# Modulation vectors 2 and 3 of the first layer: products in steps of four column groups, set into group A's projection

## The chip, the cores and the metric

One core of a Trainium2 chip. The metric is the device time of one execution in microseconds (us); lower is better. Engines: TensorE (PE; its weight loads PEld), VectorE (DVE), ScalarE (ACT), GpSimd (POOL), and SyncE (SP), on whose queue every load and store is issued, in order.

## What is computed

A two-layer transformer backbone over 512 latent tokens with 256 context tokens, width 1024, all in float32. Each layer has a mixing part (one projection whose columns feed three groups: A, a gated MLP; B, differential attention with q, k and v; C, a convolution) and a gated convolutional feed-forward part. Six modulation vectors steer a layer (shift, scale and gate, twice), for two streams: latent (`c`) and context (`c_ctx`).

```python
def adaln(cvec, w, b, n):
    m = jax.nn.silu(cvec) @ w[:, : n * D_MODEL] + b[: n * D_MODEL]
    return jnp.split(m, n, axis=-1)
...
sh1, sc1, g1, sh2, sc2, g2 = [m[:, None, :] for m in adaln(c, w_mod[l], b_mod[l], 6)]
hl = modulate(rms_norm(x_lat, norm1_g[l]), sh1, sc1)
pa, q, k, v, pc = project(hl, P, rope)
...
x_lat = x_lat + g1 * mixer_merge(pa, o, pc, P, lam_init)
h2 = modulate(rms_norm(x_lat, norm2_g[l]), sh2, sc2)
```

Vectors 0 and 1 (shift and scale of the mixing part) are needed before the projection; vector 2 (its gate `g1`) first where the output projection is added to `x`; vector 3 (shift of the second part) later still.

## The kernel before

The whole kernel is one program under a tile framework: the code names tiles, and a scheduler sets each engine's order from priorities and dependences. An engine then runs its queue in order. `low(n)` lowers the priority of what is written inside it, `tc.high_priority` raises it.

**Projections.** A matrix product in full precision is three products of rounded halves: weights and activations are split into hi and lo (`wsplit`, L215: ScalarE rounds to hi, VectorE or GpSimd subtracts for lo; `hhi`, `hlo` are the split activations). `proj_tok` (L435) projects all tokens onto 512 columns. It goes through four chunks (`k2`) of the contraction; each has two weight tiles `wh`, `wl`, and for six token tiles 24 products with `wh` (L443, L444) and then 12 with `wl` (L451), into six accumulators `acc`. After each token tile of either half it counts a step (12 a chunk, 48 in all) and calls the hooks given for that step. In the first layer the order is: group C (L486), A (L523), K, Q, V. There are two buffers each for `wh` and `wl` and three for the raw weights.

**Modulation vectors of the first layer.** `mod_rows` (L148) makes up to four pieces of 128 outputs at once on TensorE: the silu of `c` and `c_ctx` is the stationary operand `cs`, 32 columns wide (two used), the modulation weights `mraw` stream past. The eight contraction slices k go to four column groups of the array, and the results lie on four strips of 32 partitions of the accumulator `mr`:

```python
def part(o, k, w):
    r = 32 * (k % 4)
    T.matmul(o[r:r + 32], cs[:, k], w, start=k < 4, stop=k >= 4, tile_position=(0, r))
```

ScalarE copies `mr` to `mrow` (L171); four small products with `sel` (L176, tile `mt`) add the strips and turn the row into columns, and VectorE adds the bias (L181, `modv`). Vectors 0 and 1 are made in pieces of 128 columns ahead of the projection (`piece`). Vectors 2 and 3 are made behind group C in the code, in four halves of 512 columns (eight products of 512 columns, four loads of 512 KB each), under `low(RLOW)` with `RLOW = 250`: the scheduler sets each of their products among others, where it finds place. The four `mraw` buffers (`MRB`) are shared with the split weights of group A's gate (`wsh`, `wsl`, both named wmraw in the trace).

**Group A behind its projection.** ScalarE applies the gelu (L97, tiles `u`, `v`), VectorE takes mean and variance of `v` (L536), ScalarE normalises (L547), VectorE scales and shifts (L548, L549), ScalarE rounds `vbh` (L550) and VectorE makes `vbl`. `a_finish` (L553), called by hooks of K's projection, multiplies by the gate weights (tile `pg`: L275 with `vbh`, L276 with `vbl`), VectorE makes `yA` (L559), TensorE transposes it (`pt`), and ScalarE and VectorE split it.

**Beside it.** VectorE works through the convolution of group C, 60 steps (L701, tile `cacc`), at low priority. Behind K's projection it normalises and rotates the keys (`qk_tile`, from L606), splits them (`ks`), and TensorE transposes them (`pk`, L631) at hooks of Q's projection.

Of the kernel before, what the change touches and what calls it, by code (L numbers as in the profile page):

```python
# [9 lines left out]
F32 = mybir.dt.float32  # L10
# [6 lines left out]
P = 128  # L17
DM = 1024
KD = DM // P
# [10 lines left out]
COL_A, COL_Q, COL_K, COL_V, COL_C = 0, 512, 1024, 1536, 2048  # L30
# [11 lines left out]
NOSYNC = mybir.DependencyInfo(mybir.DependencyClass.NoSync, mybir.DependencyReason.DATA)  # L42
# [6 lines left out]
MRB, MRW, RAWB, NSQ, NTB, KXB, FTB = 4, 2, 3, 2, 3, 3, 2  # L49

HP, SCP, RSP = 1000, 2, 60
DLOW, RLOW = 150, 250
CLOW = (4000, 1000)

WE = "dpdpdpdddppdpppppddp"
# [21 lines left out]
def tile_backbone(  # L77
# [6 lines left out]
    nc = tc.nc  # L84
    V, S, G, T = nc.vector, nc.scalar, nc.gpsimd, nc.tensor
# [16 lines left out]
    def low(n):  # L102
        return tc.high_priority(offset=-n)
# [44 lines left out]
    def mod_rows(cs, sel, chunks, ps, tag, bufs, rp, rtag, rb):  # L148


        n = len(chunks)
        acc = ps.tile([P, 4, P], F32, tag=tag, name="mr", bufs=bufs)

        def part(o, k, w):
            r = 32 * (k % 4)
            T.matmul(o[r:r + 32], cs[:, k], w, start=k < 4, stop=k >= 4, tile_position=(0, r))  # L156

        if chunks[0][0] < 2:
            for c, (i, f) in enumerate(chunks):
                raw = rp.tile([P, KD, P], F32, tag=rtag, name="mraw", bufs=rb)  # L160
                nc.sync.dma_start(out=raw, in_=w_modN[i, f])
                for k in range(KD):
                    part(acc[:, c], k, raw[:, k])
        else:
            for k2 in range(KD // 2):
                raw = rp.tile([P, 2, 512], F32, tag=rtag, name="mraw", bufs=rb)
                nc.sync.dma_start(out=raw, in_=w_modH[chunks[0][0] - 2, chunks[0][1] // 4, k2])
                for a in range(2):
                    part(acc.rearrange("p c q -> p (c q)"), 2 * k2 + a, raw[:, a])
        mrow = rp.tile([P, 4, P], F32, tag="mrow", name="mrow", bufs=MRW)  # L170
        S.copy(mrow[:, :n], acc[:, :n])  # L171

        def finish():
            tr = ps.tile([P, 4, 2], F32, tag=tag, name="mt", bufs=bufs)
            for c in range(n):
                T.matmul(tr[:, c], mrow[:, c], sel, start=True, stop=True)  # L176
            for i in sorted({i for i, f in chunks}):
                cl = [c for c in range(n) if chunks[c][0] == i]
                f0, f1 = chunks[cl[0]][1], chunks[cl[-1]][1] + 1
                src = tr[:, cl[0]:cl[-1] + 1:(cl[1] - cl[0] if len(cl) > 1 else 1)]  # L180
                V.tensor_add(modv[:, 0, :, i, f0:f1], src.rearrange("p f s -> p s f"),  # L181
                             bmod[:, 0, i, f0:f1].unsqueeze(1).to_broadcast([P, 2, f1 - f0]))

        return finish
# [147 lines left out]
    for l in range(DEPTH):  # L332
        last = l == DEPTH - 1
        NT_KV = NLT + NCT
        NT = NLT if last else NLT + NCT
# [23 lines left out]
        with ExitStack() as ph:  # L359
            sac = ExitStack()  # L360
            sp = pool(sac, f"s1_{l}", side)
            ps = psum_pool(ph, f"ps1_{l}")
# [7 lines left out]
            def wchunk(col, k2, **kw):  # L370
                tags = ("raw", "raw") if k2 % 2 else ("hi", "lo")
                return wsplit_of(("in", col, k2), wsrc(col, k2), [2, 512], wengine(col, k2), tags, **kw)

            if l == 0:
                cs = sp.tile([P, KD, 32], F32, name="cs")
# [109 lines left out]
                    T.matmul(o.rearrange("p a n -> p (a n)"), z[:, :P], z, start=True, stop=False)  # L485
            for k2 in range(KD // 2):  # L486
                wh, wl = wchunk(COL_C, k2, raw=pre.get(k2))
                for a in range(2):
                    k = 2 * k2 + a
                    for s in range(nseg)[::-1]:  # L490
                        t0, t1 = SEG[s]
                        for m in range(4):
                            ms = slice(m * P, (m + 1) * P)
                            o = pc[s][m][:, :t1 - t0]
                            T.matmul(o, wh[:, a, ms], hhi[:, k, t0:t1], start=k == 0 and s == 0, stop=False)
                            T.matmul(o, wh[:, a, ms], hlo[:, k, t0:t1], start=False, stop=False)  # L496
                            T.matmul(o, wl[:, a, ms], hhi[:, k, t0:t1], start=False,
                                     stop=k == KD - 1 and (s == 0 or m % 2 == 1))
# [5 lines left out]
            for s in range(nseg):  # L504
                n = SEG[s][1] - SEG[s][0]
                o0 = PAD if s == 0 else 2 * PAD + LAT
                for c in range(2):
                    sg = sp.tile([P, 512], F32, tag="nsq", name="csg", bufs=2 if l else NSQ)
                    act(sg[:, :n], pc[s][2 + c][:, :n], AF.Sigmoid)
                    V.tensor_mul(cin[:, c, o0:o0 + n], pc[s][c][:, :n], sg[:, :n])  # L510
            if l == 0:
                with low(RLOW):
                    fin = []
                    for i in (2, 3):
                        for f in (0, 4):
                            fin.append(mod_rows(cs, sel, [(i, f + x) for x in range(4)], ps, "aux", 2, sp, "mraw", MRB))
                            if len(fin) > 1:
                                fin.pop(0)()
                    for f in fin:
                        f()  # L520


            pa = proj_tok(COL_A, range(NT))  # L523
            u = sp.tile([P, NT, AW], F32, name="u")
            v = sp.tile([P, NT, AW], F32, name="v")
            mv = sp.tile([P, NT, 2], F32, name="mv")
# [648 lines left out]
```

## Time and profile before

| | us |
|---|---|
| median of three runs | 1602.82 (1602.46 to 1603.99) |
| the profiled execution | 1602.73 |
| its span in the profile | 1600.4 |
| TensorE busy in it | 1565.2 |
| VectorE busy | 1016.0 |
| ScalarE busy | 643.3 |
| GpSimd busy | 113.3 |

The time is that of a whole execution; the span runs from the first to the last recorded instruction. Busy time is the union of an engine's instructions, so products that overlap count once. In a timeline row the first number is the start and the second the duration; what stands in brackets is the idle time ahead of it and what ended it. TensorE's ends are modelled, so what a product costs is read from one start to the next.

### The profile page before, as it was taken

What the parts mean: (1) busy time and instruction counts of PE and PEld (TensorE: products, weight loads), DVE (VectorE), ACT (ScalarE), POOL (GpSimd) and SP (SyncE); (2) the same over time, 40 slices, a digit from 0 to 9 for tenths busy, and PEclk for the clock granted to TensorE, in tenths of its full rate; (3) what the DMA queues carried; (4) which work ended last, traced back from release to release, by engine and by line L of the source; (5) the groups of instructions that cost most, each with busy time, mean ns of one, the idle gap of its engine ahead of it and who ended that gap; (6) DMA issues with size and microseconds to landing.
All of it is one profiled execution on the core that took longest, in us unless ns stands there. A gap on an engine that the chain in (4) does not pass through costs nothing.

```text
span 1600.4 us, 21118 instructions
## 1 busy us (share of the span) xinstructions
PE 1565.2 (98%) x8186; PEld 1289.8 (81%) x8186; DVE 1016.0 (63%) x1713; ACT 643.3 (40%) x1115; POOL 113.3 (7%) x128
## 2 busy tenths in 40 slices
PE   6999998999999999999999999999999999999999
PEld 4875776778788888888888887887778888888888
DVE  4497968969999982145444354996977444334433
ACT  5431568762532221124333233255765333123321
POOL 1130124310000000000000000001320000000000
PEclk9999999999999999999999999999999999999999
DMA  7625210015265872116666476642011323332232
GB/s 282 216 68 183 62 54 27 14 40 198 68 196 185 284 257 74 63 66 198 209 192 207 152 272 221 202 157 93 14 42 54 103 95 96 89 103 92 92 108 90
DMA packets 76372, 208.77 MB, mean 130 GB/s; under 512 B 11504, under 2 KB 13808, under 8 KB 76144
## 3 DMA queue, kind: packets, MB, share of 16 engines
q1 hardware_dynamic: 76272, 207.43, 40.0%
q8 instruction: 64, 1.05, 0.3%
q14 instruction: 36, 0.29, 0.1%
HBM read 183.28 MB, written 24.12 MB: 130 GB/s over the span
## 4 chain that ended last, share of the span: by engine, by line
PE 91%; DVE 4%; ACT 4%; issue 1%; DMA 0%; POOL 0%; POOLq 0%; DVEq 0%; SPq 0%; ACTq 0%
PE pp L276 13%; PE pp L275 13%; PE pp L277 13%; PE pd L277 6%; PE pd L276 6%; PE pd L275 6%; PE acc L443 5%; PE acc L451 5%; PE acc L444 5%; PE po L870 3%; PE wo L275 2%; PE wo L276 2%; PE wo L277 2%; PE mr L156 2%; ACT e L97 1%; PE accC L496 1%
## 5 line engine op out<-in xcount | busy, mean ns | idle before, releaser
L220 ACT CAST whi<-raw 128x1024 fp32r<-128x1024 f32 (+1 forms) x174 | 178.4, 1027 | 510.3 <-PE pp L276 248.4
L276 PE MATMUL pp<-hlo,whi 128*128 128x512 f32 (+1 forms) x1072 | 380.6, 356 | 0.8 <-DVE hlo L316 0.8
L275 PE MATMUL pp<-hhi,whi 128*128 128x512 f32 (+1 forms) x1072 | 379.8, 356 | 1.5 <-ACT whi L220 1.3
L277 PE MATMUL pp<-hhi,wlo 128*128 128x512 f32 (+1 forms) x1072 | 379.0, 355 | 0.0
L106 DVE TENSOR_TENSOR wlo<-raw,whi 128x1024 fp32r<-128x1024 f32 (+2 forms) x159 | 191.4, 1206 | 287.9 <-ACT whi L220 280.3
L275 PEld LDWEIGHTS pp<-hhi,whi 128*128 128x128 f32 x1072 | 201.3, 188 | 35.2 <-ACT whi L220 2.7
L276 PEld LDWEIGHTS pp<-hlo,whi 128*128 128x128 f32 x1072 | 201.4, 188 | 32.8 <-DVE hlo L316 1.5
L277 PEld LDWEIGHTS pp<-hhi,wlo 128*128 128x128 f32 x1072 | 201.7, 188 | 30.9
L277 PE MATMUL pd<-gh,wlo 128*128 128x512 f32 (+1 forms) x550 | 193.2, 351 | 0.0
L276 PE MATMUL pd<-gl,whi 128*128 128x512 f32 (+1 forms) x550 | 192.5, 350 | 0.0
L275 PE MATMUL pd<-gh,whi 128*128 128x512 f32 (+1 forms) x550 | 191.8, 349 | 0.0
L275 PEld LDWEIGHTS pd<-gh,whi 128*128 128x128 f32 x550 | 103.4, 188 | 15.0
L276 PEld LDWEIGHTS pd<-gl,whi 128*128 128x128 f32 x550 | 103.3, 188 | 15.1
L277 PEld LDWEIGHTS pd<-gh,wlo 128*128 128x128 f32 x550 | 103.7, 189 | 14.4
L701 DVE SCALAR_TENSOR_TENSOR cacc<-cin,cw,cacc 128x783 f32<-128x783 f32 (+1 forms) x120 | 103.4, 913 | 3.4 <-ACT cacc L696 3.4
L1037 DVE TENSOR_TENSOR ft<-ft,pp 128x256 f32<-128x256 f32 (+1 forms) x66 | 39.4, 598 | 95.9 <-PE pp L277 84.4
L192 DVE CUSTOM_DVE_ANT_0 mraw<-mraw,csil,bmod 128x1024 f32<-128x1024 f32 x64 | 81.7, 1279 | 7.2 <-DMA mraw<-in_w_modT_dram 7.1
L97 ACT ACTIVATE ft<-ft 128x768 f32<-128x768 f32 (+1 forms) x44 | 32.6, 740 | 112.4 <-DVE ft L1032 112.3
L443 PE MATMUL acc<-whi,hhi 128*128 128x512 f32 x192 | 77.7, 405 | 0.0
L444 PE MATMUL acc<-whi,hlo 128*128 128x512 f32 x192 | 77.0, 401 | 0.0
L97 ACT ACTIVATE e<-pss,mx 128x768 f32<-128x768 f32 (+1 forms) x80 | 65.1, 816 | 16.8 <-DVE mx L825 15.0
L825 DVE TENSOR_REDUCE mx<-pss 128x1 f32<-128x768 f32 (+1 forms) x80 | 67.3, 845 | 5.6 <-PE pss L823 4.6
(218 smaller groups left out, 2522.1 us busy)
## 6 DMA issues: line engine op xcount, KB each, us to landing
raw<-in_w_gv_dram SPq DMA_DIRECT2D x88, 512.0 KB, 3.2
mraw<-in_w_modT_dram SPq DMA_DIRECT2D x64, 512.0 KB, 4.3
raw<-in_w_down_dram SPq DMA_DIRECT2D x34, 512.0 KB, 3.6
wh<-in SPq DMA_DIRECT2D x24, 512.0 KB, 4.7
wl<-in SPq DMA_DIRECT2D x24, 512.0 KB, 4.5
raw<-in_w_in_dram SPq DMA_DIRECT2D x20, 512.0 KB, 3.9
araw<-in_w_in_dram SPq DMA_DIRECT2D x40, 256.0 KB, 3.6
in<-ahi SPq DMA_DIRECT2D x40, 256.0 KB, 4.7
```

Source lines behind the costliest of these rows:

```text
L97: r = S.activation(out, in_, func, **kw)
L106: (eng or V).tensor_sub(o, a, hi.bitcast(F32))
L192: r = V.tensor_tensor_reduce(out=junk, in0=w, in1=csil[:, s], scale=1.0, scalar=bmod[:, l, i, f:f + 1], op0=ALU.mult, op1=ALU.add, accum_o ...
L220: S.copy(hi, raw)
L275: T.matmul(o, lhi, rhi, start=start, stop=False)
L276: T.matmul(o, lhi, rlo, start=False, stop=False)
L277: T.matmul(o, llo, rhi, start=False, stop=stop)
L443: T.matmul(pt[t], hhi[hs], wh[:, a], start=k2 + a == 0, stop=False)
L444: T.matmul(pt[t], hlo[hs], wh[:, a], start=False, stop=False)
L451: T.matmul(pt[t], hhi[hs], wl[:, a], start=False, stop=k2 + 1 == KD // 2 and a == 1)
L701: V.scalar_tensor_tensor(out=cacc[:, c, :cn], in0=cin[:, c, j:j + cn], scalar=cw[:, l, c, j:j + 1], in1=cacc[:, c, :cn], op0=ALU.mult, op1 ...
L825: V.tensor_reduce(out=mx, in_=pss[:, :nk * P], op=ALU.max, axis=AX.X, negate=True)
```

## The change

Vectors 2 and 3 get a generator, `mod_groups`, with eight steps: two vectors, two halves of 512 columns, two halves of the contraction. A step issues four products, one for each column group, from group 3 to group 0, the last three tied behind the first, and then the loads of the step after next. After the second step of a half, ScalarE copies the accumulator (`mod_turn`, the former end of `mod_rows`), and the turning products come at the end of the next step. The generator is started, with the loads of two steps, before the last chunk of group C; the steps are hooks of group A's projection at its steps 1, 6, 12, ... 42, and the last turning at 47. `low(RLOW)` is gone. The bodies of `mod_turn` and of the copy, `mt` and `modv` are as they were.

```diff
-DLOW, RLOW = 150, 250
+DLOW = 150
+MH = (1, 6, 12, 18, 24, 30, 36, 42, 47)
...
+    def mod_groups(cs, sel, ps, tag, bufs, rp, rtag, rb):
+        todo = [(i, f, k0) for i in (2, 3) for f in (0, 4) for k0 in (0, 4)]
+        raws = {}
+        def load(x):
+            if x < len(todo):
+                i, f, k0 = todo[x]
+                raws[x] = [rp.tile([P, 2, 512], F32, tag=rtag, name="mraw", bufs=rb) for a in range(2)]
                 for a in range(2):
-                    part(acc.rearrange("p c q -> p (c q)"), 2 * k2 + a, raw[:, a])
+                    nc.sync.dma_start(out=raws[x][a], in_=w_modH[i - 2, f // 4, k0 // 2 + a])
+        load(0)
+        load(1)
+        yield
+        fin = None
+        for x, (i, f, k0) in enumerate(todo):
+            if k0 == 0:
+                acc = ps.tile([P, 512], F32, tag=tag, name="mr", bufs=bufs)
+            r = raws.pop(x)
+            head = None
+            for k in (3, 2, 1, 0):
+                c = slice(32 * k, 32 * k + 32)
+                m = T.matmul(acc[c], cs[:, k0 + k], r[k // 2][:, k % 2], start=k0 == 0, stop=k0 == 4,
+                             tile_position=(0, 32 * k))
+                if head is not None:
+                    tc.add_manual_dep(m.ins, head.name, NOSYNC, reason="next to one another")
+                head = head or m.ins
+            load(x + 2)
+            if fin:
+                fin()
+                fin = None
+            if k0 == 4:
+                fin = mod_turn(acc.rearrange("p (c q) -> p c q", q=P), [(i, f + y) for y in range(4)],
+                               sel, ps, tag, bufs, rp)
+            yield
+        fin()
+        yield
...
                 wh, wl = wchunk(COL_C, k2, raw=pre.get(k2))
+                if l == 0 and k2 == 3:
+                    mg = mod_groups(cs, sel, ps, "aux", 2, sp, "mraw", MRB)
+                    next(mg)
...
-            if l == 0:
-                with low(RLOW):
-                    fin = []
-                    for i in (2, 3):
-                        for f in (0, 4):
-                            fin.append(mod_rows(cs, sel, [(i, f + x) for x in range(4)], ps, "aux", 2, sp, "mraw", MRB))
-                            if len(fin) > 1:
-                                fin.pop(0)()
-                    for f in fin:
-                        f()
-            pa = proj_tok(COL_A, range(NT))
+            pa = proj_tok(COL_A, range(NT), [] if l else [(x, lambda: next(mg)) for x in MH])
```

How it moves the order. In the rows below, lines of the changed program are 32 to 40 higher than before (L483, L484 and L491 are L443, L444 and L451).

TensorE, the first accumulator of mr. Before, at the end of K's first chunk (`wlo_1054`), its products stand singly or by three among ordinary ones:

```order
L451 MATMUL acc_1048<-wlo_1054,hhi_93 128x512 x2
L156 MATMUL mr_710<-mraw_711,cs_106 32x512
L451 MATMUL acc_1049<-wlo_1054,hhi_93 128x512
L156 MATMUL mr_710<-mraw_715,cs_106 32x512
L451 MATMUL acc_1049<-wlo_1054,hhi_93 128x512
L156 MATMUL mr_710<-mraw_715,cs_106 32x512
L156 MATMUL mr_710<-mraw_719,cs_106 32x512 x2
L451 MATMUL acc_1050<-wlo_1054,hhi_93 128x512
L156 MATMUL mr_710<-mraw_723,cs_106 32x512
```

Now, at the end of A's first chunk (`wlo_727`), the third step with the four turning products of the half before it:

```order
L491 MATMUL acc_722<-wlo_727,hhi_93 128x512 x2
L491 MATMUL acc_723<-wlo_727,hhi_93 128x512 x2
L192 MATMUL mr_785<-mraw_740,cs_106 32x512 x2
L192 MATMUL mr_785<-mraw_739,cs_106 32x512 x2
L216 MATMUL mt_794<-sel_107,mrow_771 128x2 x4
L483 MATMUL acc_718<-whi_802,hhi_93 128x512
```

The eight products of a half now stand in two steps, the second right behind the chunk's last ordinary products. Only the first step is split, one product ahead of A's first and three behind its first token tile.

TensorE, group A's gate. Before, in the second half of K's third chunk (`wlo_1182`):

```order
L451 MATMUL acc_1047<-wlo_1182,hhi_93 128x512 x2
L451 MATMUL acc_1048<-wlo_1182,hhi_93 128x512 x2
L451 MATMUL acc_1049<-wlo_1182,hhi_93 128x512
L275 MATMUL pg_1082<-vbh_1027,wmraw_1041 128x384
L276 MATMUL pg_1082<-vbl_1028,wmraw_1041 128x384
L277 MATMUL pg_1082<-vbh_1027,wmraw_1042 128x384
L275 MATMUL pg_1091<-vbh_1027,wmraw_1041 128x384
L276 MATMUL pg_1091<-vbl_1028,wmraw_1041 128x384
L277 MATMUL pg_1091<-vbh_1027,wmraw_1042 128x384
```

Now the first two gate products stand right behind K's second chunk (`wlo_1140`), ahead of the third (`whi_1181`); those with `vbl` follow 15 ordinary products later:

```order
L491 MATMUL acc_1049<-wlo_1140,hhi_93 128x512 x2
L491 MATMUL acc_1050<-wlo_1140,hhi_93 128x512 x2
L315 MATMUL pg_1073<-vbh_1027,wmraw_1041 128x384
L315 MATMUL pg_1082<-vbh_1027,wmraw_1041 128x384
L483 MATMUL acc_1045<-whi_1181,hhi_93 128x512
L484 MATMUL acc_1045<-whi_1181,hlo_94 128x512
```

The gate begins 24 products and more earlier in K, with all its products for `vbl` still behind it.

VectorE, convolution steps up to the statistics of v (BN_STATS). Before:

```order
L701 SCALAR_TENSOR_TENSOR cacc_98<-cin_99,cw_72,cacc_98 128x783 x16
L106 TENSOR_TENSOR wlo_1054<-raw_1051,whi_1053 128x1024
L701 SCALAR_TENSOR_TENSOR cacc_98<-cin_99,cw_72,cacc_98 128x783 x6
L536 BN_STATS st6_1003<-v_985 128x6
L536 BN_STATS st6_1006<-v_985 128x6
```

Now, from the first convolution step on; `mt_794` and `mt_861` are the turning products of the first two halves:

```order
L733 SCALAR_TENSOR_TENSOR cacc_98<-cin_99,cw_72,cacc_98 128x783 x6
L108 TENSOR_TENSOR wlo_870<-raw_867,whi_869 128x1024
L221 TENSOR_TENSOR modv_67<-mt_794,bmod_68 128x2x4
L733 SCALAR_TENSOR_TENSOR cacc_98<-cin_99,cw_72,cacc_98 128x783 x11
L221 TENSOR_TENSOR modv_67<-mt_861,bmod_68 128x2x4
L733 SCALAR_TENSOR_TENSOR cacc_98<-cin_99,cw_72,cacc_98 128x783 x9
L108 TENSOR_TENSOR wlo_1054<-raw_1051,whi_1053 128x1024
L108 TENSOR_TENSOR wmraw_1042<-raw_1039,wmraw_1041 128x512
L221 TENSOR_TENSOR modv_67<-mt_924,bmod_68 128x2x4
L733 SCALAR_TENSOR_TENSOR cacc_98<-cin_99,cw_72,cacc_98 128x783 x7
L568 BN_STATS st6_1003<-v_985 128x6
```

Three of the four bias additions now stand ahead of the statistics, and six more convolution steps. From K's norm on, VectorE's order is the one before.

On SP's queue the first four loads of mraw now stand behind C's last weights and ahead of the constants and of A's first weights; the other twelve stand between the weights of A and of K.

## Rows read from the trace of the kernel before

**Rows 1.** The page, part 4: chain that ended last, share of the span by engine
```profile
PE 91%; DVE 4%; ACT 4%; issue 1%; DMA 0%; POOL 0%; POOLq 0%; DVEq 0%; SPq 0%; ACTq 0%
```

**Rows 2.** Stretch 77.78 to 168.53 us: busy time and instructions of each engine
```profile
77.78:168.53 90.75, 90.75 (x394) 59.91 (x393) 78.54 (x96) 26.14 (x45) 17.35 (x4) 1.00 0.38 123
```

**Rows 3.** Tile mr: duration min/median/max in ns, first and last start, forms
```profile
L156 PEld LDWEIGHTS mr<-mraw,cs x320: 106/110/173, 11.6 to 150.8; 128*32 128x32 f32 x160
L156 PE MATMUL mr<-mraw,cs x320: 272/273/617, 11.6 to 151.2; 128*32 128x128 f32 x128, 128*32 128x512 f32 x32
```

**Rows 4.** Timeline, TensorE: start, duration (us), then line, tile, shape, count
```profile
72.49 1.05 PE L156 MATMUL mr<-mraw,cs 128*32 128x512 f32 x2
73.47 0.51 PE L443 MATMUL acc<-whi,hhi 128*128 128x512 f32 x1
...
104.38 2.96 PE L451 MATMUL acc<-wlo,hhi 128*128 128x512 f32 x12
107.18 0.39 PE L443 MATMUL acc<-whi,hhi 128*128 128x512 f32 x1
```

**Rows 5.** Timeline, TensorE: three successive stretches of the first accumulator
```profile
116.14 1.04 PE L156 MATMUL mr<-mraw,cs 128*32 128x512 f32 x2
...
117.55 1.06 PE L156 MATMUL mr<-mraw,cs 128*32 128x512 f32 x6
...
118.96 1.04 PE L156 MATMUL mr<-mraw,cs 128*32 128x512 f32 x2
```

**Rows 6.** Timeline, TensorE: a pair in the second accumulator, between ordinary products
```profile
122.83 0.40 PE L443 MATMUL acc<-whi,hhi 128*128 128x512 f32 x1
123.16 1.05 PE L156 MATMUL mr<-mraw,cs 128*32 128x512 f32 x4
...
124.48 0.39 PE L443 MATMUL acc<-whi,hhi 128*128 128x512 f32 x1
```

**Rows 7.** Timeline, TensorE: a piece of the first two vectors
```profile
42.66 0.95 PE L176 MATMUL mt<-sel,mrow 128*128 128x2 f32 x8
43.54 0.65 PE L156 MATMUL mr<-mraw,cs 128*32 128x128 f32 x16
44.11 0.39 PE L496 MATMUL accX<-hlo,whi 128*128 128x256 f32 x1
```

**Rows 8.** Timeline, TensorE: turning products between ordinary ones
```profile
126.81 0.28 PE L176 MATMUL mt<-sel,mrow 128*128 128x2 f32 x2
...
127.26 0.28 PE L176 MATMUL mt<-sel,mrow 128*128 128x2 f32 x2
```

**Rows 9.** Timeline, ScalarE: first v of group A, and vbh
```profile
105.73 0.38 ACT L97 ACTIVATE v<-acc 128x256 f32<-128x256 f32 x1
...
126.73 1.47 ACT L550 CAST vbh<-v 128x1536 fp32r<-128x1536 f32 x1 [4.70 <-DVE v L549]
```

**Rows 10.** Timeline, VectorE, from group A's projection to K's norm
```profile
83.65 15.20 DVE L701 SCALAR_TENSOR_TENSOR cacc<-cin,cw,cacc 128x783 f32<-128x783 f32 x16
...
107.79 0.74 DVE L536 BATCH_NORM_STATS2 st<-v 128x6 f32<-128x256 f32 x2
...
121.83 3.15 DVE L701 SCALAR_TENSOR_TENSOR cacc<-cin,cw,cacc 128x783 f32<-128x783 f32 x1
...
130.46 1.75 DVE L106 TENSOR_TENSOR vbl<-v,vbh 128x1536 fp32r<-128x1536 f32 x1
...
168.53 1.27 DVE L606 TENSOR_REDUCE rk<-qsq 128x8 f32<-128x512 f32 x2
```

**Rows 11.** Timeline, TensorE: first gate product, K's last chunk, first K transposes
```profile
152.91 0.42 PE L275 MATMUL pg<-vbh,wmraw 128*128 128x384 f32 x1
...
164.76 2.96 PE L451 MATMUL acc<-wlo,hhi 128*128 128x512 f32 x12
...
176.54 0.68 PE L631 MATMUL pk<-identr,ks 128*128 128x128 f32 x6 [0.66 <-DVE ks L106]
```

**Rows 12.** DMA issues, first 200 us: KB each, median us to landing
```profile
mraw<-in_w_modH_dram SPq DMA_DIRECT2D x16, 512.0 KB, 3.9
```

More of the change, by code (lines that the diff above doesn't have):

```diff
@@ L156, in part @@
             T.matmul(o[r:r + 32], cs[:, k], w, start=k < 4, stop=k >= 4, tile_position=(0, r))
[L158 to L167, printed above, removed]
-                for a in range(2):
-                    part(acc.rearrange("p c q -> p (c q)"), 2 * k2 + a, raw[:, a])
+        for c, (i, f) in enumerate(chunks):
+            raw = rp.tile([P, KD, P], F32, tag=rtag, name="mraw", bufs=rb)
+            nc.sync.dma_start(out=raw, in_=w_modN[i, f])
+            for k in range(KD):
+                part(acc[:, c], k, raw[:, k])
@@ new lines, in mod_rows @@
+        return mod_turn(acc, chunks, sel, ps, tag, bufs, rp)
+    def mod_groups(cs, sel, ps, tag, bufs, rp, rtag, rb):
[5 more added lines that the diff above has]
+                raws[x] = [rp.tile([P, 2, 512], F32, tag=rtag, name="mraw", bufs=rb) for a in range(2)]
+                for a in range(2):
+                    nc.sync.dma_start(out=raws[x][a], in_=w_modH[i - 2, f // 4, k0 // 2 + a])
[25 more added lines that the diff above has]
+        yield
@@ L170, in mod_rows, with mod_turn @@
+    def mod_turn(acc, chunks, sel, ps, tag, bufs, rp):
+        n = len(chunks)
         mrow = rp.tile([P, 4, P], F32, tag="mrow", name="mrow", bufs=MRW)
```

## Prediction

> **What bounds the kernel now.** I read the chain that ended last first: 91% of it is TensorE, one long queue of products with hardly a gap [rows 1]. So a change pays if it shortens TensorE's own queue, unless a wait opens in its place. The table by stretches says the same of the place in question, from the first convolution step to K's norm (77.78 to 168.53 us, group A's projection and K's): TensorE is busy for all 90.75 us, while VectorE is idle for 90.75 - 78.54 = 12.2 us [rows 2]. The products of vectors 2 and 3 (tile mr) stand inside this stretch, so what they take is paid in full. I then read the timeline of TensorE for what one costs, and those of ScalarE and VectorE for who would be late next.
>
> **What the 32 products cost now.** The tile's view has their 512-column form; one product is two instructions [rows 3]. Ordinary products follow one another at (107.18 - 104.38) / 12 = 0.233 us [rows 4]. In the first accumulator a stretch of mr stands between single ordinary products: from one stretch to the next it is 117.55 - 116.14 = 1.41 us with one product in the stretch, and 118.96 - 117.55 = 1.41 us with three (x6 is six instructions) [rows 5]. Less the ordinary product, a stretch costs 1.41 - 0.233 = 1.18 us, whether it holds one product or three. A pair costs the same: from 122.83 to 124.48 us stand two ordinary products and one pair, 1.65 - 0.47 = 1.18 us [rows 6]. What costs is therefore the stretch, not the product: products in different column groups run side by side. Before, the order has 18 stretches: six of the first accumulator (the one at 72.49 us ahead of A's first product [rows 4], five around 114 to 121 us) and four pairs in each of the other three. 18 x 1.18 = 21.2 us.
>
> **What they cost after.** Nine stretches: seven of four products, and the first step split into one and three. That four run side by side is shown by the first vectors' pieces: 16 instructions, eight products of 128 columns in two rounds over the four groups, stand from 43.54 to 44.11 us, 0.57 us [rows 7]; a 512-column product alone holds 73.47 - 72.49 = 0.98 us [rows 4], so a quarter of it, twice, is 0.49 us. I take 1.18 us for a four: 9 x 1.18 = 10.6 us. **Products: -10.6 us.** Bounds for a fourth product in a stretch: nothing (as the second and third), or its two weight loads unhidden, 2 x 110 ns [rows 3], over eight stretches 1.8 us.
>
> The Trainium skill, page "TensorE: Matmul & The Clock Gate", section "Measured speedup vs the span model", speaks against full overlap: three column groups gave 2.38 times the speed of one, four row groups 3.07 times. By that a stretch of three would take 1.26 times as long as a single one, and a four (an estimate from that page) 4 / 3.07 x 0.98 = 1.28 us, 0.3 us more, or 2.4 us less gain. The trace does not agree for three: 1.41 us with three, 1.41 us with one.
>
> **The turning products (mt).** Sixteen, now mostly alone between ordinary ones: 127.26 - 126.81 = 0.45 us from one to the next, 0.22 us beyond the ordinary product [rows 8], 16 x 0.22 = 3.5 us. After, four runs of four; a piece's run takes 43.54 - 42.66 = 0.88 us [rows 7], 3.5 us. **No change.** Their input (a ScalarE copy) has 2.3 us or more of ordinary products as cover; where that cover failed, a run would wait about a microsecond.
>
> **Where A and K end.** A now takes 107.18 - 73.47 = 33.7 us with no mr inside. After, it holds eight stretches (9.4 us) and four mt runs (3.5 us) and ends at 120.1 us, T below. K now runs from 107.18 to 164.76 + 12 x 0.233 = 167.6 us [rows 4, 11], 60.4 us; freed of 17 stretches (20.1) and the mt (3.5) it takes 36.8 us and would end at 156.9 us, 10.7 us earlier, if nothing waited.
>
> **The new wait.** Group A's gate (pg) needs vbh, then vbl. Now pg starts at 152.91 us, 46 us after A's end, and waits for nothing [rows 11]. After, its first products stand right behind K's second chunk, two chunks of 36 products after A, at T + 2 x 36 x 0.233 = T + 16.8 us. The trace of before has vbh finished (126.73 + 1.47 = 128.2 us) 21.0 us after A's end and vbl (132.2 us) 25.0 us after [rows 9, 10]. Kept like that, TensorE would wait 4.2 us. But part of the lag was VectorE's backlog of convolution steps (cacc, 15.20 / 16 = 0.95 us each): the statistics of v began 0.6 us after A's end though ScalarE made the first v at 105.73 us [rows 9, 10]. After, with A 12.9 us longer, VectorE does 33 of them ahead of the statistics instead of 27 and is there when the first v is, some 2.5 us before T. What stays is 5 steps between, and a GpSimd split of K's weights that stretches a step (3.15 us at 121.83 us against 0.95 [rows 10]). ScalarE also has the fourth K chunk's rounding ahead of vbh, which waits for K's second hi half at T + 14. I get vbh at T + 16.6 with no stretched step and T + 19 with two: a wait of 0 to 2.4 us, 1.9 taken. vbl then comes 0.5 us late behind its 15 covering products, and yA and pt, three VectorE steps later, 0.4 us. **Waits: +2.8 us**, bounds 0 and 5.1 (4.2 + 0.5 + 0.4).
>
> **VectorE behind it.** From K's end on VectorE sets the pace: the first pk waits for it, 0.66 us at 176.54 us [rows 11]. So its own start on K's norm (168.53 us [rows 10]) has to move too. Up to there it does the same work after as before. Of that time 12.2 us were idle [rows 2]. After, it stands in order behind mt: it has 6 steps and a split from 77.78 us and is at the first modv at 84.7 us, whose mt ends at 86.4 (1.7 us idle); 11 steps later at 97.0 us for 98.1 (1.1); and up to 1.5 us where w_s waits for its buffer in the mraw ring. 4.3 us idle, so it gets there 7.9 us earlier at most. TensorE's 10.7 - 2.8 = 7.9 us and these 7.9 meet; where two such limits meet a little is lost, 0.5 us taken (0 to 2). **+0.5 us.**
>
> **Loads.** The 16 mraw loads move into A, two steps ahead of use: 8.4 us of A's products and two stretches, about 10 us, against 3.9 us to land [rows 12]. The first four now stand ahead of the constants and A's first weights on SP's queue and wait for the last pieces (until about 50 us), so those loads start some 7 us later, near 58 us; A starts at 73.5. No price, at worst 2 us at A's start, where VectorE's first split would be late.
>
> **Sum.** -10.6 + 2.8 + 0.5 = -7.3 us against the profiled execution's 1602.73 us, which is 0.09 us below the median shown: **1595.4 us**. Everything behind the first layer's Q projection keeps its order and moves along. A difference under 0.2% (3.2 us) cannot be told from none here.
>
> **Rivals.**
> A. No wait opens: 1592.1 us. For it: VectorE's earlier start on v. Against it: five steps stand in front of vbh and GpSimd's split falls among them. 0.12.
> B. The fours overlap partly (+1.8), or the chain to vbh keeps its 21 us (+2.3): 1597.2 to 1599.5 us. The page's rule above would belong here. 0.14.
> C. VectorE keeps most of its 12.2 us idle in new places, so that K's norm starts about when it did: 1599.5 us to no change. It needs idle time over 9 us; the two modv waits would have to be three times what I worked out. 0.10.
> D. Slower: the fours, whose order runs from group 3 down to 0, do not run side by side at all. 32 x 0.98 + 9 x 0.2 (the rest of a stretch's 1.18) = 33.2 us against 21.2: +12 us, about 1615 us. The change loses from a stretch of (21.2 - 3.3) / 9 = 2.0 us on. Against it: the stretch of three, and the pieces' 0.57 us. 0.04.
> E. The change does not do what it says: the fours are torn apart by other products. The order of the program shows only the first step torn (1 + 3), and that is in the sum.
>
> **Numbers.** My case, a gain of 5.5 to 9 us, has 0.60. Faster by over 0.2% are it, A and B: 0.86; within 0.2% C: 0.10; slower D: 0.04. The range runs from below A's 1592.1 to where C begins and a little beyond: 1591.8 to 1600.4 us.
>
> **What would show it.** In the changed kernel's profile: mr in nine stretches near 1.2 us each; A ending near 120 us; TensorE waiting for vbh at pg, 1 to 3 us; VectorE waiting for mt twice; K's norm starting near 161 us; pk waiting for VectorE as before. A stretch above 1.5 us, a pg wait above 4 us, or a wait at A's start would make it wrong.

## The result and the profile after

| | before | the change |
|---|---|---|
| median, us | 1602.88 (4 runs, 1602.46 to 1603.99) | 1593.86 (4 runs, 1593.64 to 1595.43) |
| the profiled execution, us | 1602.73 | 1593.64 |
| its span, us | 1600.4 | 1591.9 |

The ratio is 0.9945, 95% interval 0.9928 to 0.9962: faster, with the whole interval beyond the 0.2% (3.2 us) that cannot be told from no change. The forecast was 1595.4 us, the range 1591.8 to 1600.4. With the two later sets of runs of the same kernel the change has 13 runs, median 1594.45 us (1593.64 to 1596.18), and the kernel before 36 beside them, median 1602.49: 8.0 us less, against the 7.3 of the sum; the three sets by themselves give 9.0, 6.9 and 8.2 us. A run of 4377.39 us, of the later gate in experiment 5, is left out of every median and ratio.

TensorE's timeline in the changed kernel: start, duration, line, tile, shape, count, as in [rows 4].

```profile
80.89 3.06 PE L491 MATMUL acc<-wlo,hhi 128*128 128x512 f32 x12
...
91.56 1.07 PE L192 MATMUL mr<-mraw,cs 128*32 128x512 f32 x8
92.56 3.06 PE L491 MATMUL acc<-wlo,hhi 128*128 128x512 f32 x12
...
119.69 0.40 PE L483 MATMUL acc<-whi,hhi 128*128 128x512 f32 x1
```

A stretch of four products (x8, eight instructions) holds TensorE from 91.56 to 92.56, 1.00 us, where a single product held it 0.98 us [rows 4]. From the twelve products with `wlo` of one chunk to those of the next (a sweep) it is 92.56 - 80.89 = 11.67 us, with 36 ordinary products (8.40 us), two stretches and one run of mt in it. There are nine stretches, the first step torn into one and three, and K's first product comes at 119.69 us: group A ends where the prediction put it, at 120.

Then K and the gate, in the same view; what stands in brackets is the idle time ahead of the instruction and what ended it.

```profile
138.80 0.61 PE L315 MATMUL pg<-vbh,wmraw 128*128 128x384 f32 x2 [2.15 <-ACT vbh L582]
...
140.64 0.63 PE L484 MATMUL acc<-whi,hlo 128*128 128x512 f32 x1
141.07 0.63 PE L483 MATMUL acc<-whi,hhi 128*128 128x512 f32 x1
...
144.29 0.34 PE L316 MATMUL pg<-vbl,wmraw 128*128 128x384 f32 x1
...
160.65 0.40 PE L483 MATMUL acc<-whi,hhi 128*128 128x512 f32 x1
```

TensorE waits 2.15 us for vbh at pg; vbl comes in time. What the prediction did not have are the rows from 140 to 143.5 us: successive products start 141.07 - 140.64 = 0.43 us apart instead of 0.23. The table by stretches shows what goes with it. Its columns are the length, then busy time and instructions of PE, PEld, DVE, ACT and POOL, then TensorE's granted clock, DMA share and GB/s. The change first, then the kernel before:

```profile
140.00:142.00 2.00, 2.00 (x7) 1.54 (x6) 2.00 (x3) 0.00 (x0) 0.00 (x0) 0.53 0.00 0
...
254.00:256.00 2.00, 2.00 (x12) 1.63 (x13) 1.99 (x5) 1.85 (x8) 1.24 (x2) 1.00 0.00 0
```

```profile
140.00:142.00 2.00, 2.00 (x10) 0.76 (x9) 2.00 (x4) 0.01 (x1) 0.00 (x0) 1.00 0.45 137
...
254.00:256.00 2.00, 1.20 (x5) 1.24 (x6) 0.97 (x4) 1.79 (x7) 1.24 (x3) 0.50 0.00 0
```

In this execution the granted clock fell to 0.5, the 1.2 GHz level, about a microsecond behind the end of the wait; before, it was 1.00 there. About 255 us, at the start of the first attention, it is the other way round. Both places are taken up below.

VectorE and ScalarE between A's projection and K's norm, and the table for that stretch, beside [rows 10], [rows 9] and [rows 2]:

```profile
85.96 0.17 DVE L221 TENSOR_TENSOR modv<-mt,bmod 128x8 f32<-128x8 f32 x1 [0.70 <-PE mt L216]
...
97.64 0.17 DVE L221 TENSOR_TENSOR modv<-mt,bmod 128x8 f32<-128x8 f32 x1 [1.11 <-PE mt L216]
...
119.33 0.17 DVE L221 TENSOR_TENSOR modv<-mt,bmod 128x8 f32<-128x8 f32 x1 [0.26 <-PE mt L216]
...
120.22 3.00 DVE L733 SCALAR_TENSOR_TENSOR cacc<-cin,cw,cacc 128x783 f32<-128x783 f32 x1
...
132.35 3.17 DVE L733 SCALAR_TENSOR_TENSOR cacc<-cin,cw,cacc 128x783 f32<-128x783 f32 x1
135.44 1.75 DVE L581 TENSOR_TENSOR v<-v,lnv 128x1536 f32<-128x1536 f32 x1
...
144.83 1.14 DVE L591 SCALAR_TENSOR_TENSOR yA<-pg,bst,u 128x384 f32<-128x384 f32 x2 [1.06 <-PE pg L317]
...
161.31 1.27 DVE L638 TENSOR_REDUCE rk<-qsq 128x8 f32<-128x512 f32 x2
```

```profile
137.28 1.47 ACT L582 CAST vbh<-v 128x1536 fp32r<-128x1536 f32 x1 [2.29 <-DVE v L581]
```

```profile
77.78:161.31 83.53, 81.38 (x389) 60.26 (x388) 77.63 (x96) 25.33 (x45) 12.04 (x4) 0.98 0.37 128
```

VectorE waits for mt three times (0.70, 1.11, 0.26 us), two of its convolution steps are stretched to 3.00 and 3.17 us beside GpSimd's splits, and vbh follows the second of them. VectorE is now idle for 83.53 - 77.63 = 5.9 us, 1.06 of it at yA, behind the slow products. It starts K's norm at 161.31 instead of 168.53 us.

### The profile page after: what moved, and what is told of

It is laid out like the page before. It is cut to its first block, busy times and chain, and to the rows that moved or that the text cites. A ratio compares the mean times of both kernels' runs of the same rounds, so it can differ in the third digit from the quotient of the medians.

```text
span 1591.9 us, 21110 instructions
## 1 busy us (share of the span) xinstructions
PE 1555.6 (98%) x8186; PEld 1287.7 (81%) x8186; DVE 1015.4 (64%) x1713; ACT 643.0 (40%) x1115; POOL 108.0 (7%) x128
## 4 chain that ended last, share of the span: by engine, by line
PE 75%; DVE 2%; ACT 1%; issue 0%; POOLq 0%; DVEq 0%; ACTq 0%
PE pp L316 13%; PE pp L315 13%; PE pp L317 13%; PE pd L315 6%; PE pd L317 6%; PE pd L316 6%; PE acc L483 2%; PE acc L484 2%; PE acc L491 2%; PE wo L315 2%; PE wo L316 2%; PE wo L317 2%; PE po L902 1%; PE accC L540 0%; PE accC L538 0%; PE accC L539 0%
## 5 line engine op out<-in xcount | busy, mean ns | idle before, releaser
L483 PE MATMUL acc<-whi,hhi 128*128 128x512 f32 x192 | 78.5, 409 | 0.0
L484 PE MATMUL acc<-whi,hlo 128*128 128x512 f32 x192 | 76.6, 399 | 0.0
```

The costliest lines, as they stand in the source:

```text
L483: T.matmul(pt[t], hhi[hs], wh[:, a], start=k2 + a == 0, stop=False)
L484: T.matmul(pt[t], hlo[hs], wh[:, a], start=False, stop=False)
```

## The experiments

**Theory:** what costs is the stretch, 1.17 us whatever it holds of up to four products, so nine fewer stretches give the gain, less the new wait at the gate. **Rivals:** the products cost, not the stretches; the new place of the products gives the gain; VectorE's queue sets the pace behind A, so that what TensorE saves is partly lost there.

**1. The change once more.** No edit.

> The changed kernel as it is, for a second profile. Two pieces of its gain are not yet told apart: 7.3 us that are there when K's norm begins (the fewer stretches, less the gate's wait), and 1.65 us that come later, where the kernel before ran at half the granted clock from 252 to 260 us and the changed one did not. If that clock piece belongs to the program's timing, this profile shows full clock there again and a time near 1593.9 us. If it is chance from execution to execution, the profile may show half clock at the start of the attention, and the span is then some 1.6 us longer (about 1593.5 instead of 1591.9).

Measured: 1595.48 us (1594.34 to 1596.18), ratio 0.9956 (0.9941 to 0.997). Its profile is the cleaner one to hold against the sum:

```profile
73.44 0.50 PE L483 MATMUL acc<-whi,hhi 128*128 128x512 f32 x1
...
139.31 0.62 PE L315 MATMUL pg<-vbh,wmraw 128*128 128x384 f32 x2 [2.15 <-ACT vbh L582]
139.77 0.39 PE L483 MATMUL acc<-whi,hhi 128*128 128x512 f32 x1
140.00 0.40 PE L484 MATMUL acc<-whi,hlo 128*128 128x512 f32 x1
...
143.03 0.39 PE L483 MATMUL acc<-whi,hhi 128*128 128x512 f32 x1
143.40 0.44 PE L316 MATMUL pg<-vbl,wmraw 128*128 128x384 f32 x1
...
159.88 0.40 PE L483 MATMUL acc<-whi,hhi 128*128 128x512 f32 x1
...
168.53 0.59 PE L663 MATMUL pk<-identr,ks 128*128 128x128 f32 x5
```

```profile
144.21 1.13 DVE L591 SCALAR_TENSOR_TENSOR yA<-pg,bst,u 128x384 f32<-128x384 f32 x2
...
160.54 1.27 DVE L638 TENSOR_REDUCE rk<-qsq 128x8 f32<-128x512 f32 x2
```

```profile
140.00:142.00 2.00, 2.00 (x10) 1.64 (x9) 2.00 (x3) 0.00 (x0) 0.00 (x0) 1.00 0.00 0
...
248.00:250.00 2.00, 2.00 (x8) 1.64 (x7) 1.58 (x7) 1.39 (x5) 0.47 (x1) 0.50 0.00 0
```

The wait for vbh is the same 2.15 us, but behind it products follow at 140.00 - 139.77 = 0.23 us, and VectorE does not wait at yA. Here the clock falls where it fell before the change, at the start of attention. Counted from A's first product:

| us | before | the change | once more |
|---|---|---|---|
| A's first product at | 73.47 | 72.91 | 73.44 |
| K's first product | +33.71 | +46.78 | +46.76 |
| K's last product ends | +94.09 | +87.74 | +86.44 |
| K's norm on VectorE | +95.06 | +88.40 | +87.10 |
| first pk | +103.07 | +96.39 | +95.09 |
| span | 1600.4 | 1591.9 | 1592.6 |

Two profiles with the clock fall in the same place differ by 7.96 us at K's norm, 7.98 at the first pk and 7.8 in the span: the whole gain is made between A's start and K's norm, and kept. In the first profile of the change the fall behind the gate costs 88.40 - 87.10 = 1.3 us, and its lead over before grows from 168.53 - 161.31 = 7.2 us to 350.63 - 341.65 = 9.0 us (an ACT table load in both), because there the attention starts at full clock. The second is nothing that the edit brings, as the repeat shows; the first is a chance that came in with the new wait (below).

**2. Each four torn into two pairs,** 17 stretches with the same 32 products, in the same place.

```diff
-MH = (1, 6, 12, 18, 24, 30, 36, 42, 47)
+MH = (1, 3, 6, 9, 12, 15, 18, 21, 24, 27, 30, 33, 36, 39, 42, 45, 47)
...
                 head = head or m.ins
+                if k == 2:
+                    yield
+                    head = None
```

> Each step of four is torn into two pairs, three token steps apart: 17 stretches instead of 9, the same 32 products. Theory (a stretch costs 1.18 us whether it holds one, two or four products): 8 x 1.18 = 9.4 us more in group A, which then ends near 128.5 us instead of 119.6; VectorE gets further ahead meanwhile, so the gate's wait of 2.15 us goes or shrinks, and the time is 1593.9 + 7 to 9.4 = 1601 to 1603 us. Rival (the products themselves cost, 32 x about 0.3 us, wherever they stand): no more than 1 us longer, 1594 to 1595 us.

Measured: 1604.35 us (10 runs), ratio 1.0013 (1.0004 to 1.0023), 8.9 us over the change run beside it: inside the 7 to 9.4 us expected, though above the 1601 to 1603 us, which were counted from the change's first median.

```profile
81.01 1.05 PE L192 MATMUL mr<-mraw,cs 128*32 128x512 f32 x4
81.99 1.66 PE L494 MATMUL acc<-wlo,hhi 128*128 128x512 f32 x6
...
95.99 1.66 PE L494 MATMUL acc<-wlo,hhi 128*128 128x512 f32 x6
```

```profile
148.32 0.61 PE L318 MATMUL pg<-vbh,wmraw 128*128 128x384 f32 x2 [2.43 <-ACT vbh L585]
```

A sweep now takes 95.99 - 81.99 = 14.00 us instead of 11.67, for two stretches more: 1.165 us each. A pair holds TensorE from 81.01 to 81.99, 0.98 us, a four 1.00. TensorE waits for nothing inside A in either kernel. So the stretch costs and not the product, and eight stretches take the whole gain away. One point missed: the wait for vbh did not shrink but stood at 2.43 us. A ends later, and what waits at the gate hangs on A's end: vbh is done 19.06 us after K's first product in the change, 19.33 here, and 19.05 both in experiment 3 and in the eights of experiment 7, where A ends at other times.

**3. Half of the fours issued twice,** back to back; the first round of each is overwritten.

```diff
-            for k in (3, 2, 1, 0):
+            for d, k in [(d, k) for d in range(1 if k0 else 2) for k in (3, 2, 1, 0)]:
...
-start=k0 == 0, stop=k0 == 4,
+start=k0 == 0, stop=k0 == 4 or (d == 0 and k0 == 0),
```

> The fours of the first contraction half are issued twice, one round right behind the other (the first round closed and overwritten): 16 more products in four of the stretches and no more stretches. If four column groups run side by side, a second four adds its streaming alone, 0.85 to 1.0 us: mr takes 3.4 to 4 us more in group A, and the time is 1593.9 + 1.5 to 4 us, since the gate's wait can shrink by up to 2.15 us. If the fours run partly one behind the other, each adds 1.3 us or more, over 5 us; if wholly, 16 x 0.98 = 15.7 us.

Measured: 1599.69 us (10 runs), ratio 0.9983 (0.9974 to 0.9993), 4.2 us over the change run beside it, a little more than the 1.5 to 4 us expected.

```profile
82.02 3.06 PE L491 MATMUL acc<-wlo,hhi 128*128 128x512 f32 x12
85.00 1.92 PE L192 MATMUL mr<-mraw,cs 128*32 128x512 f32 x16
86.86 1.05 PE L216 MATMUL mt<-sel,mrow 128*128 128x2 f32 x8
...
94.53 3.06 PE L491 MATMUL acc<-wlo,hhi 128*128 128x512 f32 x12
```

A stretch of two fours lasts 86.86 - 85.00 = 1.86 us against 1.00; a sweep takes 94.53 - 82.02 = 12.51 instead of 11.67 us, 0.84 more. So of a stretch's 1.17 us some 0.84 are streaming, in which four products go side by side, and 0.33 are paid once a stretch. Had the four run one behind another, the second round would have cost about four times as much. Four such stretches are 3.4 us; what the other 0.8 us are stays open. The wait at the gate, which could have shrunk, is 2.15 us here too.

**4. The fours in the old place,** behind the first convolution's inputs, where the order spreads them mostly over K.

```diff
+            if l == 0:
+                with low(RLOW):
+                    for _ in mod_groups(cs, sel, ps, "aux", 2, sp, "mraw", MRB):
+                        pass
...
-            pa = proj_tok(COL_A, range(NT), [] if l else [(x, lambda: next(mg)) for x in MH])
+            pa = proj_tok(COL_A, range(NT))
```

> The steps of four are written where the old code stood, behind group C at low priority, and not hung on group A's steps: most land in K's projection. The order has 12 stretches (the first half torn, the other three halves in fours) instead of 18 before and 9 in the change; group A is not lengthened and its gate comes late again. Theory (stretches pay, the place costs the gate's wait and saves VectorE idle time): 6 x 1.18 = 7.1 us less TensorE work than before, no wait at the gate, 1602.9 - 7.1 = 1595.8 us if VectorE follows, and up to 1600 us if VectorE keeps its idle time and K's transposes wait for it. Rival (the gain comes from the place, not from the fours): no change from before, 1602 to 1603 us.

Measured: 1596.16 us (4 runs), ratio 0.996 (0.9945 to 0.9975), 0.7 us over the change run beside it.

```profile
146.51 0.42 PE L315 MATMUL pg<-vbh,wmraw 128*128 128x384 f32 x1
...
169.91 0.68 PE L665 MATMUL pk<-identr,ks 128*128 128x128 f32 x6 [0.65 <-DVE ks L108]
```

The order makes 12 stretches of them there. The gate waits for nothing, and pk waits 0.65 us for VectorE, as it did before [rows 11]. K's norm comes 88.26 us after A's first product, 6.8 us sooner than before; six stretches less at 1.17 are 7.0. So the fours give the gain and not the place. The new place saves three stretches more and pays two thirds of that back at the gate.

**5 to 8. Four attempts on the wait,** in this order: group A's gate asked for later (its start in AH from step 4 to 28; in the order its first products then come six ordinary products later); the modv additions of vectors 2 and 3 on GpSimd; eights instead of fours; all three.

```diff
-AH = ((4, 1), (18, 1))
+AH = ((28, 1), (18, 1))
...
-                V.tensor_add(modv[:, 0, :, i, f0:f1], src.rearrange("p f s -> p s f"),
+                    mc = rp.tile([P, 4, 2], F32, tag="mc", name="mc", bufs=2)
+                    S.copy(mc, tr)
+                    G.tensor_add(modv[:, 0, :, i, f0:f1], mc.rearrange("p f s -> p s f"), bm)
...
-MH = (1, 6, 12, 18, 24, 30, 36, 42, 47)
+MH = (6, 6, 18, 18, 30, 30, 42, 42, 47)
```

Later gate: 

> The gate's hooks start 24 token steps later in K's projection, so that its products stand behind the third chunk's first half, some 4 us later, when vbh is there. Theory (VectorE sets the pace: K's norm waits for VectorE, not for TensorE): the wait of 2.15 us at the gate goes, but K's norm starts within 0.7 us of the same distance from A's first product (87.1 and 88.4 us in the two profiles of the change), TensorE waits at the first K transposes instead, and the time changes by less than 0.7 us. Rival (the gate's wait is on the path): the time falls by 2.15 us and K's norm comes 2 us earlier.

GpSimd: 

> The four bias additions of vectors 2 and 3 leave VectorE: ScalarE copies the turned products, GpSimd adds. VectorE loses its two waits for mt (0.70 and 1.11 us). Theory: it then stands idle the longer ahead of the statistics of v, which wait for A's end (it is there 0.73 us early now), so vbh and the gate's wait stay within 0.5 us of what they are; behind, nothing but the four short additions is saved, and the time changes by less than 0.7 us. Rival (the idle time in front of mt is lost for good): 1.8 us faster.

Eights: 

> Both steps of a half stand at one token step (at the end of a chunk's first half): four stretches of eight products and the one product that goes ahead of A, instead of nine stretches. TensorE: 9 x 1.18 = 10.6 us becomes 1.18 + 4 x 2.04 = 9.3 us, less what a turning run saves inside a stretch: 1.3 to 2 us less in group A. If TensorE's queue in A is what counts, the time falls by 1.3 to 2 us. If VectorE's backlog counts (theory), it is late for the statistics of v by about as much as A got shorter, the gate's wait grows, and 0.3 to 1 us is left.

All three: 

> Eights, bias additions off VectorE and the late gate together. If the three limits (TensorE in A, VectorE's waits for mt, the gate's place) only hide one another, the sum is more than its parts: VectorE's two waits (1.8 us) are used because A is shorter, and the gate does not wait: 2 to 3 us faster than the change, 1592 us. If each is lost again to VectorE's backlog ahead of K's norm: within 1 us of the change.

| | median, us | ratio to before | at the gate | K's norm after A's first product |
|---|---|---|---|---|
| later gate | 1594.04 (3 runs) | 0.9945 (0.9926 to 0.9965) | vbl 2.32, then clock 0.50 | 88.68 |
| modv on GpSimd | 1593.80 | 0.9952 (0.9937 to 0.9966) | vbh 1.10, vbl 0.43 | 86.40 |
| eights | 1594.15 | 0.9949 (0.9935 to 0.9964) | vbh 2.15, then clock 0.50 | 87.79 |
| all three | 1594.71 | 0.9953 (0.9938 to 0.9967) | vbl 1.27 | 86.42 |

The timelines, of the later gate, of modv on GpSimd (TensorE, then VectorE), and of all three (TensorE):

```profile
143.12 0.44 PE L316 MATMUL pg<-vbl,wmraw 128*128 128x384 f32 x1 [2.32 <-DVE vbl L108]
```

```profile
138.54 0.62 PE L320 MATMUL pg<-vbh,wmraw 128*128 128x384 f32 x2 [1.10 <-ACT vbh L587]
```

```profile
85.97 18.99 DVE L738 SCALAR_TENSOR_TENSOR cacc<-cin,cw,cacc 128x783 f32<-128x783 f32 x20
108.18 1.23 DVE L108 TENSOR_TENSOR wlo<-raw,whi 128x1024 fp32r<-128x1024 f32 x1 [3.21 <-issue]
...
122.32 2.37 DVE L738 SCALAR_TENSOR_TENSOR cacc<-cin,cw,cacc 128x783 f32<-128x783 f32 x1
```

```profile
142.56 0.44 PE L321 MATMUL pg<-vbl,wmraw 128*128 128x384 f32 x1 [1.27 <-DVE vbl L108]
```

The later gate only exchanges the wait for vbh for one for vbl. With modv elsewhere VectorE runs 20 steps through where it stood before mt twice, but that time is not won: it then stands idle for 3.21 us ahead of a weight split (0.24 in the change) and for 0.78 us ahead of the statistics of v (0.73). vbh is a microsecond sooner by what comes behind: no third wait for mt (0.26 us and the addition), and a stretched step of 2.37 us where the change has 3.00. K's norm is 0.7 us sooner than in experiment 1. The eights are torn by the mt run into fours again (only the first stretch holds seven) and save 0.6 us: K's norm is at 87.79 us against 88.40 in the change's first profile, where the clock falls behind the wait too; with all three together their faster use of the ring also makes TensorE wait 0.29 and 0.40 us for mraw loads. None of the four can be told from the change by its ratio to the kernel before (the change itself, 0.9945 to 0.9956 in its three sets, was not run beside them); the gain of 2 to 3 us that was expected of all three together did not come.

**9 to 11. The gate behind K's third chunk,** 8.4 us of products later, alone and with modv on GpSimd, beside the change a third time.

```diff
-AH = ((4, 1), (18, 1))
+AH = ((36, 1), (18, 1))
```

Third chunk: 

> Group A's gate moved from behind K's second chunk to behind its third, 8.4 us of products later; nothing else changed, nine stretches of four. Both theories: TensorE waits for neither vbh nor vbl, and K's last product ends 2.3 us sooner after A's first product than in the repeat of the change (86.44 us there, 84.2 here). Theory 1, the wait for vbh sets K's norm: K's norm starts 84.7 to 85.5 us after A's first product (87.1 in the repeat, 88.4 in the first profile of the change). Theory 2, VectorE's own queue sets it and the wait is only the slack of TensorE: K's norm stays at 86.3 to 87.1 us, the first pk waits for VectorE by 1.5 to 2.5 us, and the median stays within 1 us of the change run beside it. On the clock: four of the six profiles that had a wait of 2.1 us or more at the gate show TensorE's granted clock at 0.5 for some 4 us behind it, none of the four others does; if the wait is what brings it, this kernel shows 1.00 from 132 to 160 us, and the median gains up to 1.3 us by that alone.

With modv on GpSimd: 

> As the kernel with the gate behind K's third chunk, with the additions that make vectors 2 and 3 taken from VectorE and put on GpSimd behind a ScalarE copy, so VectorE no longer stands in order behind the turning products. Theory 1: no further gain at K's norm, 84.7 to 85.5 us after A's first product. Theory 2: VectorE's two waits of 0.7 and 1.1 us go, K's norm starts 0.7 us sooner than without that (as it did with the gate in its old place, 86.4 against 87.1 us), and the median falls by 0 to 1 us against the change.

The change: 

> The change unchanged, a third profile and more runs of it on the chip of the two others. Both theories: nine stretches, the wait for vbh at 2.15 us, median 1594 to 1596 us. On the clock behind the wait: either 1.00 throughout (K's norm 87.1 us after A's first product) or a fall to 0.5 for some 4 us (88.4 us); the fall behind the wait and the one at about 245 to 260 us each cost 1.3 to 1.7 us.

Measured: third chunk 1597.47 us (5 runs), ratio 0.9965 (0.9953 to 0.9978); with modv on GpSimd 1598.90 (9 runs), 0.9975 (0.9965 to 0.9985); the change 1594.45 (5 runs), 0.9948 (0.9935 to 0.996). Third chunk alone, VectorE, TensorE and the table by stretches:

```profile
142.34 5.75 DVE L733 SCALAR_TENSOR_TENSOR cacc<-cin,cw,cacc 128x783 f32<-128x783 f32 x6
...
149.15 1.13 DVE L591 SCALAR_TENSOR_TENSOR yA<-pg,bst,u 128x384 f32<-128x384 f32 x2
```

```profile
149.81 0.45 PE L315 MATMUL pg<-vbh,wmraw 128*128 128x384 f32 x1 [2.26 <-DVE yA L591]
...
170.22 0.77 PE L663 MATMUL pk<-identr,ks 128*128 128x128 f32 x7 [1.28 <-DVE ks L108]
```

```profile
152.00:154.00 2.00, 2.00 (x7) 1.71 (x6) 1.85 (x3) 0.00 (x0) 0.00 (x0) 0.50 0.81 303
```

With modv on GpSimd, TensorE and the table:

```profile
169.83 0.76 PE L668 MATMUL pk<-identr,ks 128*128 128x128 f32 x7 [2.69 <-DVE ks L108]
```

```profile
172.00:174.00 2.00, 2.00 (x6) 1.52 (x6) 2.00 (x6) 1.58 (x4) 0.00 (x0) 0.50 0.00 0
```

Both theories missed. vbh and vbl are there in time, but VectorE, whose order follows the gate's place, now has six convolution steps and a split standing between vbl and yA, so the third pg waits 2.26 us for yA to free its buffer, the clock falls behind that wait, and the first pk waits 1.28 us. It comes 97.70 us after A's first product, 2.6 us later than in the third profile of the change (95.12), and the median is 3.0 us higher. The wait was not removed but moved. With modv on GpSimd the wait for yA is 1.20 us and the clock holds there, but the first pk waits 2.69 us; it comes 1.4 us later than in the third profile of the change, and the clock falls behind this wait. At the ACT table load near 345 us the profile is 3.1 us behind the change's, counted from A's first product, as is the third chunk alone; its span is 3.2 us longer. So the wait at pk and the fall behind it make up what this profile loses. The median is 4.5 us higher; the profiled execution is the fastest of its nine. The change's own profile has 87.13 us at K's norm and 1.00 behind the wait, as in experiment 1.

**The clock behind the wait.** Eight of the thirteen profiles show TensorE waiting 2.1 us or more for one of vbh, vbl or yA at the gate. In five the granted clock then falls to about 0.5 for some 4 us (the change, twice, later gate, eights, third chunk), in three it does not (once more, pairs, third profile). In the five without such a wait it never falls there, but in one of them (third chunk with modv on GpSimd) it falls behind the 2.69 us at pk. The same program did it once in three times, so a wait of this size does not force the fall, and no profile has a fall between 100 and 200 us without one; what decides is open. No version was faster than the change by more than can be measured.

**The third rival.** In the change's three profiles the first pk waits for nothing, so VectorE's queue costs it nothing there. It is close to the limit: the waits at pk are 0.43 to 0.66 us in the later gate, with modv on GpSimd and in all three together, and 1.28 and 2.69 us with the gate behind the third chunk.

## Why the prediction was right

Point by point, with the profile of experiment 1, whose clock is like that of before:

- **Stretch, 1.18 us whatever it holds:** right. 1.165 us for each stretch more (experiment 2), and the bound of 1.8 us for two more weight loads was not needed: a four holds TensorE 0.02 us longer than a pair. The Trainium skill, page "TensorE: Matmul & The Clock Gate", section "Measured speedup vs the span model", has four row groups at 3.07 times one in its table, which gave an estimate of 1.28 us for a four; the trace, of four column groups, does not agree, with 1.00 us.
- **A ends at 120.1 us:** right, 46.76 us after its first product (predicted 46.6).
- **K takes 36.8 us without waits:** 0.6 us short. 86.44 - 46.76 = 39.68 us, less the waits (2.3 us, below) 37.4; where the 0.6 us lie stays open.
- **mt no change:** fits the sweep: 11.67 - 8.40 - 2 x 1.165 = 0.94 us for a run of four, 0.88 taken.
- **Wait for vbh 1.9 us:** right in mechanism and nearly in size, 2.15. In the first profile vbh is done 137.28 + 1.47 - 119.69 = 19.1 us after A's end, the 19 worked out for two stretched steps, and two steps are stretched (3.00 and 3.17 us). That GpSimd's splits stretch them is argued from their standing beside each other; no run tests it.
- **vbl 0.5, yA and pt 0.4:** too much. vbl cost 143.40 - 143.03 - 0.23 = 0.14 us, pt nothing. Waits are 2.3 instead of 2.8.
- **VectorE 4.3 us idle:** 82.76 - 78.08 = 4.7, by the table below. The pieces are not all those of the prediction: 1.74 and 1.11 us up to the first two modv (1.7 and 1.1 predicted), but 0.36 at w_s, where up to 1.5 was put, and 0.99 ahead of the statistics and at a third mt that it did not have.

```profile
77.78:160.54 82.76, 80.61 (x391) 59.45 (x390) 78.08 (x96) 25.85 (x45) 12.05 (x4) 1.00 0.38 131
```

- **0.5 us lost where the two limits meet:** did not come. K's norm starts 7.96 us sooner, a little more than K's end (94.09 - 86.44 = 7.65). With it goes most of the 0.7 us between forecast and gain. That the rest is so near is in part luck: K took 0.6 us more than in the sum and the waits 0.5 us less, which cancel. pk no longer waits for VectorE in any of the change's three profiles, where the prediction had it waiting as before.
- **Loads at no price:** right. A starts 0.03 to 0.56 us earlier in the three profiles, and no mraw load is late.
- **Rivals:** A (no wait) fell to the 2.15 us; B to the 1.00 us of a four and to vbh, which comes 19.1 and not 21 us after A's end; C to 4.7 us idle; D to the 1.00 us too, and to experiment 3; E to the nine stretches.
- **Left out:** the granted clock. Behind the new wait it can fall, 1.3 us in the change's first profile. The trace of before has 1.00 in all that stretch; but at the first attention it shows 0.50 behind three waits of TensorE of 0.69 to 0.90 us, so a fall behind the new wait could have stood in the sum as a chance.

## What to carry to other kernels

Small products that use a quarter of the array's columns cost by the stretch here, not by the product: put those of different column groups together before looking for a better place, and count the stretches in the order the program really has. When such work moves to an earlier stage, work out which wait takes its place and what sets it: here one engine's backlog was worth 2.2 us, and moving the waiting step later only brought the next step of that backlog into view. Compare profiles from a landmark ahead of the change, and look at the granted clock in both, before giving a difference of one or two microseconds a cause.

## What was not expected of the hardware

- The clock fell at the start of the first attention, to 0.5 for 6 to 8 us, in some executions of one program and not in others: of the change's three profiles the first has 1.00 there and the others 0.50, though TensorE's waits up to there are alike (0.79, 0.90 and 0.69 us in the first, 0.80, 0.90 and 0.69 in the second). The lead of that first profile grows by 1.8 us over it. Of all thirteen profiles four have no fall there; three of these had fallen behind the gate (the change, twice, later gate), but eights and both third chunks fell in both stages, so whether the two are linked is open. The fourth, all three together, has 1.00 in both and the shortest span, 1590.8 us.
- Of a stretch's 1.17 us, 0.33 are paid once whether it holds one round of four products or two (experiment 3). Some 0.2 of it lie in its neighbours: before, the ordinary product ahead of a stretch takes 123.16 - 122.83 = 0.33 us to the next start [rows 6] instead of 0.233, and the one behind it is as slow, 1.65 - 0.33 - 0.98 = 0.34 us (0.98 is the pair).
